# A 4096 x 4096 matmul with bias and tanh by two levels of seven products: returned blocks of the third column in another order, and the last pair's sums in another form

## The chip, the cores and the metric

One core of a Trainium2 chip. The metric is the device time of the kernel in microseconds. The kernel before took 1517.2 us, the median of 3 runs (1516.6 to 1518.86).

## What is computed

```python
def setup_inputs():
    m, k, n = 4096, 4096, 4096
    return {
        "a": np.random.randn(m, k).astype(np.float32),
        "b": np.random.randn(k, n).astype(np.float32),
        "bias": np.random.randn(n).astype(np.float32),
    }

def reference(a, b, bias):
    return np.tanh(np.matmul(a, b) + bias)
```

## The kernel before

**Tiling.** The output is cut into four columns of 1024 (`c` = 0 to 3) and sixteen pairs of row blocks of 128. For a pair and a column, A is a 2 x 2 of quadrants (a11, a12, a21, a22: row block by half of the K axis) and so is B (b11, b12, b21, b22: half of K by half of the column). The product is formed in the way of Strassen and Winograd, with seven products m1 to m7 of half size in place of eight, on sums of quadrants: m2 takes b11, m5 b22, m3 d3, m4 d4, m1 d1, m6 e6, m7 e7 on the right (`PRODUCTS`). Each right operand of a column lies in SBUF as four blocks, 0 to 3, of 512 KB. All operands are fp16, sums are fp32 in eight PSUM banks (named ps), TensorE does the products, VectorE the sums of operands and of results, ScalarE copies, clears of banks and the tanh.

**The second level.** In the columns 2 and 3, `four(n)` takes two pairs at once, p and q, and forms every product but m1 by seven quarter products again. Their right operands, called t1 to t4 and the quarters themselves, are "forms" of 512 KB. For m3, m4, m5 and m7 they stay in SBUF: t3 is written over a quarter, (0, 1), of the operand itself (blocks 0 and 1, the right halves), and what stood there is first moved to DRAM (tiles away_...). For m2 and m6 all forms lie in DRAM and are streamed by GpSimd's queue into a few buffers (the tags b11_1 to b11_3, e6_2, e6_3 and a spare): when `multiply` has used one, `let_go` frees its buffer and `pull_four` issues the next load, which waits for TensorE. Within `four`, `group0`, `group1` and `single` are the quarter products in the order of writing: `single(..., 7)`, `3` and `4` are the last three of a product. `group1` returns two adds (`w`, `w2` or `u`, `u2`) that add a shared third, x or o (an SBUF copy of a PSUM half bank), to the right half banks of p and q.

**Leaving.** The last pair of pairs in column 2 (`leave`) forms m1, m6 and m7 whole, 16 products of 512 columns each, and is followed by two steps of ordinary items of column 2 and then by column 3. For these, what was displaced has to come back: the moved quarters (`move(..., False, ...)`, SyncE's queue, two pieces of 256 KB each, tiles d3, d4, b22 and e7), the blocks of b11 and e6, whose buffers had held forms (`bring_block`, GpSimd's queue, two pieces of 256 KB a block; block 0 of both lies in the tile `side`), and b12 and b21 of the next column (`load_raw`, GpSimd's queue, from the fp16 copy in DRAM, 512 KB a block). The table `BACK` says at which `step(k)` of the leaving pair each is issued: step 1 stands after `group0` of m3 and m4, 5 after m4's last product, 6 after m3's, 8 after `group1` of m2 and m5 and the fetches of a22, 10 after m5's last product, 11 and 12 after the first and second m1, 14 to 17 after m6 and m7 of p and of q, and 18 and on in the slots of the items that follow. Blocks of b11 and e6 that are not in the table come back at once when `let_go` frees their buffer.

**Order.** Every engine runs its instructions in the order of writing, so the place of a line in `four` sets what stands ahead of it on each queue. SyncE's queue carries fetches of A, returned quarters and the stores of results; GpSimd's carries forms, blocks and B. The result buffers `ds` and `s` (two each) are taken anew by `take_d` and `take_c`, which must wait until the store of the pair before has read them. `seed` clears a half bank with ScalarE once VectorE has taken what it held, and the next product adds onto it.

**The last pair.** At the end of column 3 `w2` and `u2` add the third to q's right half bank, `first_half` then adds q's left half of the sum into PSUM and the right half into SBUF, applies tanh and stores; `w`, `take_m6` and `u`, `take_m7` do the same for p with 512 columns; the last two products, `single(n, what, 4)`, are followed by a tanh of q's left half straight from PSUM and its store.

Of the kernel before, what the change touches and what calls it, by code (L numbers as in the profile page):

```python
# [20 lines left out]
ADD = mybir.AluOpType.add  # L21
SUB = mybir.AluOpType.subtract
MUL = mybir.AluOpType.mult
TANH = mybir.ActivationFunctionType.Tanh
# [68 lines left out]


BACK = {
# [3 lines left out]
}  # L99

PLACE = {
# [6 lines left out]
HALF = (ds(0, NB // 2), ds(NB // 2, NB // 2))  # L108
# [14 lines left out]
def kernel(  # L123
# [7 lines left out]
    nc = tc.nc  # L131
# [20 lines left out]
    def tt(out_, in0, in1, op):  # L152
        nc.vector.tensor_tensor(out=out_, in0=in0, in1=in1, op=op)  # L153
# [6 lines left out]
    def bank(n, s, what):  # L160
        two = items[n][2] is not None
        if what == "w":
            return banks[5 + 2 * (n % 2)]
        if what == "z":
            return banks[4 + 2 * (n % 2) + (s if two else 0)]
        return banks[(0 if what == "d" else 2) + (s if two else n % 2)]
# [157 lines left out]
    def by_four(x):  # L324
        return x if len(x.shape) == 4 else x.rearrange("p (a b) m -> p a b m", b=TB)
# [171 lines left out]
    def new_out():  # L497
        return outs.tile([P, NB], fp32, name="o", tag="o")
# [314 lines left out]
    def bring_block(c, name, blk):  # L813
        if (c, name, blk) not in blocks:
            what = {"b11": "m2", "e6": "m6"}[name]
            r, i = divmod(blk, 2)
            to = new_bop(name, blk)
            for j in range(2):
                there = corners[name, blk] if (r, j) == (0, 1) else forms[what, (r, j)][:, ds(i * TB, TB)]
                nc.gpsimd.dma_start(out=to[:, :, HALF[j]], in_=there)  # L820
            return
        nc.gpsimd.dma_start(out=new_bop(name, blk), in_=blocks[c, name, blk])

    owner = {}
    free, held, placed, left_count, homes, returned = [], {}, {}, [0], {}, []
# [9 lines left out]
    def let_go(what, name):  # L835
        tag = held.pop((what, name))
        if returned and not queue and tag != "sum":
            bring_block(returned[0], tag[:-2], int(tag[-1]))
        else:
            free.append(tag)  # L840
        pull_four()

    def half_of(n, what, h):
        return by_four(aset[n][TWO[what][0]])[:, ds(h * TP // TB, TP // TB)]
# [12 lines left out]
    def left(n, what, name):  # L857
        of = {"v2": "v1", "v4": "v2"}.get(name)
        if of:
            assert (what, of) in owner.values()  # L860
            of = by_four(placed[what, of])
        place = by_four(place_for(n, what, name))
        if name == "v1":
            tt(place, half_of(n + 1, what, 0), half_of(n + 1, what, 1), SUB)
        elif name == "v2":
            tt(place, half_of(n, what, 0), of, SUB)
        elif name == "v3":
            tt(place, half_of(n + 1, what, 0), half_of(n, what, 0), SUB)
        else:
            tt(place, half_of(n, what, 1), of, SUB)  # L870
# [28 lines left out]
    def third(src, spread=False):  # L899
        if spread:  # L900
            x = new_out()[:, ds(0, NB // 2)]
        else:
            x = halves.tile([P, NB // 2], fp32, name="x", tag="x")
        nc.scalar.copy(x, src)
        return x

    def group0(n, what):
        p, q = pair_of(n, what)
        multiply(n, what, p[:, HALF[0]], (0, 0), (0, 0))
        nc.scalar.copy(p[:, HALF[1]], p[:, HALF[0]])  # L910
        multiply(n, what, between(n, what), "v1", "t1")

    def group1(n, what, spread=False):
        p, q = pair_of(n, what)
        multiply(n, what, p[:, HALF[0]], (0, 1), (1, 0))
        multiply(n, what, p[:, HALF[1]], "v2", "t2")
        nc.scalar.copy(q[:, HALF[0]], p[:, HALF[1]])
        x = third(between(n, what), spread)
        return (
            lambda: tt(p[:, HALF[1]], p[:, HALF[1]], x, ADD),  # L920
            lambda: tt(q[:, HALF[1]], q[:, HALF[0]], x, ADD),
        )

    def single(n, what, *numbers):
        p, q = pair_of(n, what)
        for i in numbers:
            if i == 3:
                multiply(n, what, p[:, HALF[1]], "v4", (1, 1))
            else:
                multiply(n, what, q[:, HALF[0]], *(("v3", "t3") if i == 7 else ((1, 1), "t4")))  # L930
# [62 lines left out]
    def four(n):  # L993
        c = items[n][0]
        p, q, m = n, n + 1, n + 2
# [4 lines left out]
        st = {i: state.setdefault((i, 0), {}) for i in (p, q)}  # L1000
# [19 lines left out]
        def end(name, i, r, j):  # L1020
            nc.scalar.activation(st[i][name], st[i][name], TANH)
            store(st[i][name], pair[i], r, c, j)
# [24 lines left out]
        def take_m6(i, anew=False, later=False):  # L1047
            tt(st[i]["s"], st[i]["s"], bank(i, 0, "w"), ADD)
            if anew:
                seed(i, "w", 0)  # L1050
            if later:
                left_over.append(lambda: end("s", i, 1, 1))
            else:
                end("s", i, 1, 1)

        def take_m7(i, anew=False, later=False):
            tt(st[i]["ds"], st[i]["ds"], bank(i, 0, "z" if leave else "d"), SUB)
            if anew:
# [21 lines left out]
        w, w2 = group1(n, "m4")  # L1080
# [3 lines left out]
        u, u2 = group1(n, "m3", True)  # L1084
# [35 lines left out]
        w, w2 = group1(n, "m2")  # L1120
# [9 lines left out]
        u, u2 = group1(n, "m5", True)  # L1130
# [73 lines left out]
        w, w2 = group1(n, "m6")  # L1204
# [6 lines left out]
        u, u2 = group1(n, "m7", True)  # L1211
        if not last:
            fetch(m, "a12")
        less_m1(q)
        left(n, "m7", "v4")
        if last:
            parts = {"m6": ("s", "w", ADD, 1.0, 1), "m7": ("ds", "d", SUB, -1.0, 0)}

            def first_half(what):
                name, at, op, scale, r = parts[what]  # L1220
                o, here = st[q][name], bank(q, 0, at)
                tt(here[:, HALF[0]], here[:, HALF[0]], o[:, HALF[0]], op)
                tt(o[:, HALF[1]], o[:, HALF[1]], here[:, HALF[1]], op)
                nc.scalar.activation(o[:, HALF[1]], o[:, HALF[1]], TANH)
                store_half(o, q, r, 1, nc.sync)

            single(n, "m6", 7)
            w2()
            first_half("m6")
            single(n, "m7", 7)  # L1230
            u2()
            first_half("m7")
            single(n, "m6", 3)
            w()
            take_m6(p)
            single(n, "m7", 3)
            u()
            take_m7(p)
            for what in ("m6", "m7"):
                name, at, op, scale, r = parts[what]  # L1240
                single(n, what, 4)
                o = st[q][name]
                nc.scalar.activation(o[:, HALF[0]], bank(q, 0, at)[:, HALF[0]], TANH, scale=scale)
                store_half(o, q, r, 0, nc.sync if what == "m6" else nc.scalar)
            return
        single(n, "m6", 7)
        w2()
        single(n, "m7", 7)
# [334 lines left out]
    def load_first(m, queue, out_):  # L1583
# [9 lines left out]
        out=ident, in_=ident, compare_op=mybir.AluOpType.is_equal, fill=0.0,  # L1593
# [45 lines left out]
    ends = {}  # L1639
# [94 lines left out]
    for c in range(1, NC):  # L1734
        n = next(n for n in range(len(items)) if items[n][0] == c)
# [55 lines left out]
    for n in partner:  # L1791
# [26 lines left out]
        if by_two(n, "m4"):  # L1818
# [5 lines left out]
            at = 9 if by_two(n, "m6") else 8  # L1824
# [8 lines left out]
    for slot in range(1 - len(ORDER), SLOTS * len(items)):  # L1833
# [14 lines left out]
        for pos, p in PRODUCTS.items():  # L1848
            n, r = divmod(slot - pos, SLOTS)
# [37 lines left out]
```

## Time and profile before

| | us |
|---|---|
| median of 3 runs | 1517.2 |
| the profiled execution | 1517.48 |
| its span | 1515.7 |
| TensorE busy in the span | 1506.1 |
| leaving pair of column 2, from the stores of the pair before to the last whole product | 1056 to 1105 |
| last pair of column 3, from the last sums to the last store | 1506 to 1514 |

In the groups and timelines of the profile a row gives engine, line, operation, the tile written and the tiles read, the shapes (partitions x elements) and the number of instructions; in a timeline the start and the length in us stand first, and in brackets the idle time ahead of it and what ended that. A row of the windows gives, for a stretch of the span, its length and the busy time and number of instructions of PE (TensorE), PEld (its weight loads), DVE (VectorE), ACT (ScalarE) and POOL (GpSimd), then the granted clock of TensorE, the busy share of the sixteen DMA engines and GB/s. SPq and POOLq are the queues in which SyncE and GpSimd issue transfers. Buffer numbers are left out: `b` stands for any block of b11, b12, b21 or b22, `d` for d1, d3 or d4, `e` for e6 or e7, `h` for a left operand of a quarter product, `g` and `form` for forms.

### The profile page before, as it was taken

Reading aid. Unit: us, or ns where it says so; the run is one execution under the profiler, and the core shown is the slowest. Engines: PE = TensorE matmul, PEld = TensorE weight load, DVE = VectorE, ACT = ScalarE, POOL = GpSimd, SP = SyncE. Lnnn points to the kernel's source line nnn. Section 1 sums busy time; section 2 is a strip of 40 time slices with the busy share of each in tenths; the row PEclk is TensorE's granted clock in tenths of the full one; section 3 lists DMA queues with packets and bytes.
Section 4 is the critical chain, followed back from the end, with each engine's and each line's share of the span. In section 5 each row is a group of like instructions: output and inputs, shape, how many; then the busy total and the mean of one; then the engine's idle time right before and its main releaser. Section 6 shows DMA issues by size and latency. Waiting matters only on the chain.

```text
span 1515.7 us, 23996 instructions
## 1 busy us (share of the span) xinstructions
PE 1506.1 (99%) x9101; PEld 889.4 (59%) x9101; DVE 1184.5 (78%) x1646; ACT 380.3 (25%) x830; POOL 494.0 (33%) x889
## 2 busy tenths in 40 slices
PE   9999999999999999999999999999999999999998
PEld 4444444444445566544444578888644458888886
DVE  6789877777876666677787888889658879888888
ACT  4431111111221122111122223333212222333332
POOL 8775443433603231343453311112312121111111
PEclk9999999999999999999999999999999999999999
DMA  9999998999979998999998978898976687888895
GB/s 185 178 208 257 269 261 213 215 214 241 187 219 287 268 277 267 232 253 238 244 172 243 304 269 302 325 339 300 363 251 204 202 285 266 304 307 314 320 337 181
DMA packets 207672, 390.39 MB, mean 258 GB/s; under 512 B 25538, under 2 KB 103874, under 8 KB 207556
## 3 DMA queue, kind: packets, MB, share of 16 engines
q0 software_dynamic: 119616, 203.22, 57.6%
q1 hardware_dynamic: 87268, 185.24, 34.9%
q8 instruction: 71, 1.16, 0.3%
q10 hardware_dynamic: 672, 0.39, 0.1%
q14 instruction: 45, 0.37, 0.1%
HBM read 337.65 MB, written 136.84 MB: 313 GB/s over the span
## 4 chain that ended last, share of the span: by engine, by line
PE 96%; DMA 2%; POOL 1%; DVE 1%; issue 0%; ACT 0%; SPq 0%; DVEq 0%; POOLq 0%
PE ps L478 56%; PE ps L895 26%; PE ps L957 6%; PE ps L1516 5%; PE ps L678 4%; DMA out_dram<-ds 1%; DMA out_dram<-o 1%; DMA b<-in_b_dram 0%; DMA land<-in_a_dram 0%; POOL side L1605 0%; POOL land L1557 0%; DVE ps L153 0%; DVE h L153 0%; POOL first L1585 0%; DVE ds L153 0%
## 5 line engine op out<-in xcount | busy, mean ns | idle before, releaser
L478 PEld LDWEIGHTS <-a 128*128 128x128 f16 x3136 | 306.7, 98 | 365.1 <-DMA a<-scratch 0.5
L478 PE MATMUL ps<-b,a 128*128 128x512 f16 x1092 | 249.2, 379 | 0.1
L895 PEld LDWEIGHTS <-h 128*128 128x128 f16 x2176 | 212.7, 98 | 27.4 <-DVE h L153 0.9
L833 POOL DMA_DIRECT2D form<-form_m x147 | 77.8, 530 | 407.6 <-PE ps L895 365.2
L478 PE MATMUL ps<-d,a 128*128 128x512 f16 x896 | 202.5, 379 | 0.0
L478 PE MATMUL ps<-e,a 128*128 128x512 f16 x876 | 199.3, 379 | 0.0
L278 DVE STREAM_TRANSPOSE a<-nat 128x1024 f16<-128x1024 f16 (+2 forms) x202 | 175.3, 912 | 19.1 <-PE ps L478 17.6
L895 PEld LDWEIGHTS <-a 128*128 128x128 f16 x1632 | 159.6, 98 | 26.5 <-issue 2.1
L478 PE MATMUL ps<-d,s 128*128 128x512 f16 x624 | 141.0, 379 | 0.0
L250 POOL DMA_DIRECT2D nat<-in_a_dram x176 | 93.0, 533 | 132.0 <-DVE a L278 63.6
L478 PEld LDWEIGHTS <-s 128*128 128x128 f16 x816 | 79.9, 98 | 94.1
L381 POOL DMA_DIRECT2D b<-in_b_dram x192 | 103.5, 545 | 84.0 <-DVE a L278 31.0
L153 DVE TENSOR_TENSOR a<-a,a 128x2048 f16<-128x2048 f16 (+1 forms) x103 | 123.9, 1202 | 0.2
L895 PE MATMUL ps<-form,h 128*128 128x256 f16 x848 | 108.1, 273 | 0.1
L153 DVE TENSOR_TENSOR h<-a,h 128x1024 f16<-128x1024 f16 x136 | 92.3, 685 | 12.5 <-PE ps L895 12.3
L502 ACT ACTIVATE o<-ps 128x512 f32<-128x512 f32 x88 | 52.9, 601 | 152.3 <-issue 101.8
L895 PE MATMUL ps<-form,a 128*128 128x256 f16 x672 | 83.6, 273 | 0.1
L957 PE MATMUL ps<-d,a 128*128 128x512 f16 x352 | 79.4, 379 | 0.0
L153 DVE TENSOR_TENSOR ds<-ds,ps 128x512 f32<-128x512 f32 (+1 forms) x100 | 66.8, 679 | 10.6 <-PE ps L957 5.5
L979 ACT CAST ps<-zeros 128x256 f32<-128x256 f16 x140 | 50.1, 380 | 98.7 <-DVE s L153 51.5
L153 DVE TENSOR_TENSOR ps<-ps,x 128x256 f32<-128x256 f32 x90 | 38.7, 430 | 41.9 <-PE ps L895 26.8
L478 PE MATMUL ps<-side,a 128*128 128x512 f16 x272 | 69.8, 379 | 0.0
(196 smaller groups left out, 1934.8 us busy)
## 6 DMA issues: line engine op xcount, KB each, us to landing
form<-form_m POOLq DMA_DIRECT2D x147, 512.0 KB, 7.4
a<-scratch SPq DMA_DIRECT2D x140, 512.0 KB, 7.2
out_dram<-o SPq DMA_DIRECT2D x199, 256.0 KB, 5.8
nat<-in_a_dram POOLq DMA_DIRECT2D x288, 128.0 KB, 6.5
scratch<-a SPq DMA_DIRECT2D x48, 512.0 KB, 6.6
b<-in_b_dram POOLq DMA_DIRECT2D x160, 128.0 KB, 5.6
scratch<-a SPq DMA_DIRECT2D x32, 256.0 KB, 6.2
cast<-in_b_dram POOLq DMA_DIRECT2D x64, 128.0 KB, 9.4
```

The lines of the kernel that those rows point to most:

```text
L153: nc.vector.tensor_tensor(out=out_, in0=in0, in1=in1, op=op)
L250: nc.gpsimd.dma_start(out=tl[ds(q * QP, QP), :, :], in_=src.rearrange("(mb p) k -> p mb k", p=QP),)
L278: nc.vector.transpose(dst[:, ds(b0 * tb, n * tb), :].rearrange("P (b t) (mb p) -> P mb b t p", t=tb, p=QP), src[:, :, ds(b0, n), :].rearra ...
L381: nc.gpsimd.dma_start(out=dst[ds(q * QP, QP), ds(t, nt)], in_=src)
L478: nc.tensor.matmul(st[where], at, bt, start=(what == "m2" or n < LEAD and what == "m1") and i == 0, stop=i == len(ts_) - 1, skip_group_che ...
L502: nc.scalar.activation(o, src, TANH)
L678: nc.tensor.matmul(to, at, bt, start=False, stop=t == TP - 1, skip_group_check=True)
L833: nc.gpsimd.dma_start(out=rights[what, name], in_=forms[what, name])
L895: nc.tensor.matmul(to, at, bt, start=False, stop=t == TP - 1, skip_group_check=True)
L957: nc.tensor.matmul(to[:, half], at[:, t // TB, t % TB], bop[right, t // TB][:, t % TB, half], start=anew and t == 0, stop=t == T - 1, skip ...
L979: nc.scalar.copy(bank(n, 0, where)[:, HALF[half]], zeros)
L1516: nc.tensor.matmul(mb[m % 4, j], aq[m, kt // T][:, kt % T, :], right(kt, j), start=fresh and kt == k0, stop=stop and kt == k1 - 1, skip_gr ...
```

## The change

The table gets other steps, and two more entries, blocks 2 and 3 of b11, which `let_go` therefore no longer brings back by itself. In the last pair the shared thirds, kept in a dictionary, are added by GpSimd to the right halves of the sums in SBUF, for q and p, ahead of the last products; p's left halves are added by themselves, early; and the adds that remain take only the half bank that the last product wrote.

```diff
 BACK = {
-    ("m4", "t3"): 5, ("m3", "t3"): 12, ("m7", "t3"): 1,
-    ("b12", 0): 12, ("b12", 1): 12, ("b21", 0): 18, ("b21", 1): 18,
-    ("b11", 0): 6, ("e6", 0): 2, ("e6", 1): 5, ("m5", "t3"): 12,
+    ("m4", "t3"): 17, ("m3", "t3"): 16, ("m7", "t3"): 8,
+    ("b12", 0): 17, ("b12", 1): 17, ("b21", 0): 19, ("b21", 1): 19,
+    ("b11", 0): 9, ("e6", 0): 6, ("e6", 1): 7, ("m5", "t3"): 10, ("b11", 2): 10, ("b11", 3): 11,
 }
...
     def let_go(what, name):
         tag = held.pop((what, name))
         if returned and not queue and tag != "sum":
-            bring_block(returned[0], tag[:-2], int(tag[-1]))
+            name, blk = tag[:-2], int(tag[-1])
+            if (name, blk) not in BACK:
+                bring_block(returned[0], name, blk)
         else:
             free.append(tag)
...
+    thirds = {}
+
...
-        x = third(between(n, what), spread)
+        x = thirds[what] = third(between(n, what), spread)
...
         less_m1(q)
-        left(n, "m7", "v4")
         if last:
-            parts = {"m6": ("s", "w", ADD, 1.0, 1), "m7": ("ds", "d", SUB, -1.0, 0)}
+            ends = {"m6": ("s", "w", ADD, 1.0, 1), "m7": ("ds", "d", SUB, -1.0, 0)}
+            near, far = HALF
+            for what, (name, at, op, scale, r) in ends.items():
+                for i in (q, p):
+                    o = st[i][name][:, far]
+                    nc.gpsimd.tensor_tensor(out=o, in0=o, in1=thirds[what], op=op)
+
+            def take(what, i, half, src):
+                name, at, op, scale, r = ends[what]
+                tt(st[i][name][:, half], st[i][name][:, half], src, op)
+
+            for what, (name, at, op, scale, r) in ends.items():
+                take(what, p, near, bank(p, 0, at)[:, near])
+                if what == "m6":
+                    left(n, "m7", "v4")
+            for what, (name, at, op, scale, r) in ends.items():
                 o, here = st[q][name], bank(q, 0, at)
-                tt(here[:, HALF[0]], here[:, HALF[0]], o[:, HALF[0]], op)
-                tt(o[:, HALF[1]], o[:, HALF[1]], here[:, HALF[1]], op)
-                nc.scalar.activation(o[:, HALF[1]], o[:, HALF[1]], TANH)
+                single(n, what, 7)
+                take(what, q, far, here[:, near])
+                tt(here[:, near], here[:, near], o[:, near], op)
+                nc.scalar.activation(o[:, far], o[:, far], TANH)
                 store_half(o, q, r, 1, nc.sync)
-
-            single(n, "m6", 7)
-            w2()
-            first_half("m6")
-            single(n, "m7", 7)
-            u2()
-            first_half("m7")
-            single(n, "m6", 3)
-            w()
-            take_m6(p)
-            single(n, "m7", 3)
-            u()
-            take_m7(p)
-            for what in ("m6", "m7"):
-                name, at, op, scale, r = parts[what]
+            for what, (name, at, op, scale, r) in ends.items():
+                single(n, what, 3)
+                take(what, p, far, bank(p, 0, at)[:, far])
+                end(name, p, r, r)
+            for what, (name, at, op, scale, r) in ends.items():
                 single(n, what, 4)
                 o = st[q][name]
-                nc.scalar.activation(o[:, HALF[0]], bank(q, 0, at)[:, HALF[0]], TANH, scale=scale)
+                nc.scalar.activation(o[:, near], bank(q, 0, at)[:, near], TANH, scale=scale)
                 store_half(o, q, r, 0, nc.sync if what == "m6" else nc.scalar)
             return
+        left(n, "m7", "v4")
```

TensorE's instructions and their order are the same in both kernels. The queues show what the table moves. On SyncE's queue, at the start of the leaving pair (out_0_dram is a store of the pair before, away_m7 and away_m4 are returned quarters), before:

```order
L493 DMA out_0_dram<-ds_9201 128x512
L493 DMA out_0_dram<-ds_9189 128x512
L493 DMA out_0_dram<-s_9226 128x512
L644 DMA e7_0_6535<-away_m7_2_t3_6891 128x4x256
L644 DMA e7_1_6567<-away_m7_2_t3_6891 128x4x256
L644 DMA d4_0_6513<-away_m4_2_t3_6856 128x4x256
L644 DMA d4_1_6537<-away_m4_2_t3_6856 128x4x256
L312 DMA a22_9828<-scratch_15_107 128x1024
```

and with the change:

```order
L493 DMA out_0_dram<-ds_9201 128x512
L493 DMA out_0_dram<-ds_9189 128x512
L493 DMA out_0_dram<-s_9226 128x512
L312 DMA a22_9822<-scratch_15_107 128x1024
L312 DMA a22_9822<-scratch_14_106 128x1024
L312 DMA a22_9827<-scratch_15_107 128x1024
L312 DMA a22_9827<-scratch_14_106 128x1024
L644 DMA e7_0_6535<-away_m7_2_t3_6891 128x4x256
L644 DMA e7_1_6567<-away_m7_2_t3_6891 128x4x256
```

m7's quarter moved behind the four fetches of a22; m4's stands 20 rows further down, behind the last store of `ds`, m3's four rows ahead of it, and m5's between the stores of m5's results.

On GpSimd's queue in the same place (form_9595 is the last form whose load the pair before releases, side and e6_1 are blocks 0 and 1 of e6), before:

```order
L833 DMA form_9595<-form_m2_4_6824 128x2048
L820 DMA side_108<-form_m6_0_7014 128x4x256
L820 DMA side_108<-corner_e6_0_6984 128x4x256
L820 DMA e6_1_9726<-form_m6_0_7014 128x4x256
L820 DMA e6_1_9726<-corner_e6_1_7047 128x4x256
L833 DMA form_9753<-form_m2_5_6886 128x2048
L833 DMA form_9764<-form_m2_6_6859 128x2048
```

and with the change:

```order
L833 DMA form_9595<-form_m2_4_6824 128x2048
L833 DMA form_9744<-form_m2_5_6886 128x2048
L833 DMA form_9755<-form_m2_6_6859 128x2048
L820 DMA side_108<-form_m6_0_7014 128x4x256
L820 DMA side_108<-corner_e6_0_6984 128x4x256
L820 DMA e6_1_9791<-form_m6_0_7014 128x4x256
L820 DMA e6_1_9791<-corner_e6_1_7047 128x4x256
L820 DMA e6_2_9803<-form_m6_2_7089 128x4x256
```

The two blocks moved behind two forms; further down block 0 of b11 goes behind its block 1, and the next column's b21 behind its first two blocks of b11.

On VectorE at the end of the program (s and ds are the sums in SBUF, 14067 and 14030 p's, 14078 and 14042 q's; h is the last left operand; x and o are the thirds), before:

```order
L153 TENSOR_TENSOR h_10767<-a12_13829,h_10767 128x1024
L153 TENSOR_TENSOR ps_1_248<-ps_1_248,x_14324 128x256
L153 TENSOR_TENSOR ps_1_248<-ps_1_248,s_14078 128x256
L153 TENSOR_TENSOR s_14078<-s_14078,ps_1_248 128x256
L153 TENSOR_TENSOR ps_6_253<-ps_6_253,o_14345 128x256
L153 TENSOR_TENSOR ps_6_253<-ps_6_253,ds_14042 128x256
L153 TENSOR_TENSOR ds_14042<-ds_14042,ps_6_253 128x256
L153 TENSOR_TENSOR ps_3_250<-ps_3_250,x_14324 128x256
L153 TENSOR_TENSOR s_14067<-s_14067,ps_3_250 128x512
L153 TENSOR_TENSOR ps_0_247<-ps_0_247,o_14345 128x256
L153 TENSOR_TENSOR ds_14030<-ds_14030,ps_0_247 128x512
```

and with the change:

```order
L153 TENSOR_TENSOR s_14067<-s_14067,ps_3_250 128x256
L153 TENSOR_TENSOR h_10767<-a12_13829,h_10767 128x1024
L153 TENSOR_TENSOR ds_14030<-ds_14030,ps_0_247 128x256
L153 TENSOR_TENSOR s_14078<-s_14078,ps_1_248 128x256
L153 TENSOR_TENSOR ps_1_248<-ps_1_248,s_14078 128x256
L153 TENSOR_TENSOR ds_14042<-ds_14042,ps_6_253 128x256
L153 TENSOR_TENSOR ps_6_253<-ps_6_253,ds_14042 128x256
L153 TENSOR_TENSOR s_14067<-s_14067,ps_3_250 128x256
L153 TENSOR_TENSOR ds_14030<-ds_14030,ps_0_247 128x256
```

Four adds of x and o have left VectorE; they are the last four instructions of GpSimd, behind its last form. p's left halves stand around the last `h`, and p's two adds of 512 became 256.

More of the change, by code (lines that the diff above doesn't have):

```diff
@@ L1214, in four @@
         less_m1(q)
-        left(n, "m7", "v4")
         if last:
-            parts = {"m6": ("s", "w", ADD, 1.0, 1), "m7": ("ds", "d", SUB, -1.0, 0)}
-            def first_half(what):
-                name, at, op, scale, r = parts[what]
+            ends = {"m6": ("s", "w", ADD, 1.0, 1), "m7": ("ds", "d", SUB, -1.0, 0)}
[4 more added lines that the diff above has]
+                    nc.gpsimd.tensor_tensor(out=o, in0=o, in1=thirds[what], op=op)
@@ L1231, in four @@
-            u2()
-            first_half("m7")
-            single(n, "m6", 3)
-            w()
-            take_m6(p)
-            single(n, "m7", 3)
-            u()
-            take_m7(p)
-            for what in ("m6", "m7"):
-                name, at, op, scale, r = parts[what]
+            for what, (name, at, op, scale, r) in ends.items():
[3 more added lines that the diff above has]
+            for what, (name, at, op, scale, r) in ends.items():
```

## The prediction

> **What bounds the kernel now.** I read the page's head first, then a table of equal windows, then TensorE's waits, and last the timelines of the two places that the diff touches.
>
> ```profile
> span 1515.7 us, 23996 instructions
> PE 1506.1 (99%) x9101; PEld 889.4 (59%) x9101; DVE 1184.5 (78%) x1646; ACT 380.3 (25%) x830; POOL 494.0 (33%) x889
> ...
> 1040.00:1080.00 40.00, 38.40 (x329) 31.87 (x328) 31.07 (x50) 13.05 (x36) 12.82 (x20) 1.00 0.99 349
> 1080.00:1120.00 40.00, 39.73 (x200) 19.21 (x198) 20.41 (x30) 7.93 (x14) 8.40 (x14) 1.00 1.01 352
> ...
> 1480.00:1520.00 40.00, 30.33 (x247) 23.88 (x244) 28.75 (x46) 9.95 (x25) 4.23 (x8) 0.95 0.50 171
> ...
> PE ps L895 <- ACT ps L979: 1.5, 1, 1.5
> ```
>
> TensorE is busy 1506.1 of 1515.7 us at a granted clock of 1.00, and the change leaves its instructions and their order as they were. So a gain can come only from TensorE's gaps. After the opening, nearly all of them lie in two places: 1.60 + 0.27 us in the third column's leaving pair (1040 to 1120), and the tail, where TensorE ends near 1510.33 and the span at 1515.7. Both parts of the diff sit exactly there.
>
> **The leaving pair: what is lost there.** A busy share hides the slow restart of a pipelined TensorE, so I measure the loss against the pair one earlier, which runs the same products in the same order. Rows of that pair, then of the leaving pair:
>
> ```profile
> 1013.33 1.04 PE L895 MATMUL ps<-d,a 128*128 128x256 f16 x8
> 1027.34 1.04 PE L895 MATMUL ps<-b,a 128*128 128x256 f16 x8
> 1037.82 3.62 PE L957 MATMUL ps<-d,a 128*128 128x512 f16 x16
> ...
> 1056.95 1.04 PE L895 MATMUL ps<-d,a 128*128 128x256 f16 x8
> 1072.63 1.03 PE L895 MATMUL ps<-b,a 128*128 128x256 f16 x8 [1.51 <-ACT ps L979]
> 1083.89 7.07 PE L957 MATMUL ps<-d,a 128*128 128x512 f16 x32
> ```
>
> From the first of these groups to the last the earlier pair takes 1037.82 - 1013.33 = 24.49 us and the leaving pair 1083.89 - 1056.95 = 26.94. The loss is 2.45 us, 1.67 of it before m5's first product (15.68 against 14.01), the rest in restarts and in a late VectorE behind it. Why was m5 late?
>
> ```profile
> 1057.28 3.76 SPq L493 DMA_DIRECT2D out_dram<-ds  x2
> 1061.72 2.34 SPq L644 DMA_DIRECT2D e<-away_m_t  x2
> 1065.11 5.08 SPq L644 DMA_DIRECT2D d<-away_m_t  x2
> ...
> 1057.28 14.11 DMA out_dram<-ds
> ...
> 1024.32 0.69 DVE L153 TENSOR_TENSOR ds<-ps,bias_bc 128x512 f32<-128x512 f32 x1
> 1071.48 0.69 DVE L153 TENSOR_TENSOR ds<-ps,bias_bc 128x512 f32<-128x512 f32 x1 [3.66 <-DMA out_dram<-ds]
> ...
> 1024.00:1026.00 2.00, 2.00 (x21) 1.80 (x19) 1.87 (x5) 0.58 (x2) 0.00 (x0) 1.00 0.11 43
> 1068.00:1070.00 2.00, 2.00 (x21) 1.79 (x20) 0.00 (x0) 0.00 (x0) 0.32 (x1) 1.00 1.03 377
> ```
>
> VectorE's take_d needs a `ds` buffer whose store to DRAM was issued at 1057.28 and took 14.11 us. ScalarE clears the bank behind take_d, m5 waits for the clearing. One pair earlier the same add starts at 1024.32; moved by the distance of the pairs (1056.95 - 1013.33 = 43.62) that is 1067.94, and here it is 1071.48. The last two rows (busy times, then clock, DMA share, GB/s) show why: at that point the earlier pair's DMA engines have run dry (0.11), here they are full (1.03), with four quarters on SyncE's queue and the four pieces of e6's blocks 0 and 1 on GpSimd's, 8 x 256 KB.
>
> **Step 1, the table BACK.** It moves just these eight out of the time before 1069: m7's quarter behind the fetches of a22, m4's and m3's behind the m7 products, e6's blocks behind the last two forms, and those wait for TensorE:
>
> ```profile
> 1069.68 0.55 POOL L833 DMA_DIRECT2D form<-form_m  x1 [7.79 <-PE ps L895]
> ```
>
> Between 1057 and 1069 the queues then hold what they held one pair earlier, so I take the earlier pair as the price: take_d at about 1068, no gap, **2.45 us gained**. Bounds: nothing, if the store is as slow without them; above, 2.6, since a later start is at stake too:
>
> ```profile
> 1090.80 1.03 PE L957 MATMUL ps<-side,a 128*128 128x512 f16 x4
> 1098.57 6.21 PE L957 MATMUL ps<-e,a 128*128 128x512 f16 x28
> 1104.80 1.04 PE L478 MATMUL ps<-side,a 128*128 128x512 f16 x4
> 1100.17 1.84 SPq L312 DMA_DIRECT2D a<-scratch  x4
> ```
>
> 32 products of this form run in 6.91 us (1083.89 to 1090.80, where the next group starts), so 28 should end at 1104.61; the next starts 0.19 late, on a21, fetched only at 1100.17. Two quarters stood ahead of that fetch on SyncE and are now behind it. I count nothing for it.
>
> What is late next? Eight 256 KB pieces now go out after 1069.7, beside what already went there. The first users stand 2.45 us earlier than now, and a product of 16 takes 3.45: e6's block 0 at 1088.35 (1090.80 - 2.45), e7 with m7's quarter one product on at 1091.8, b11 at 1102.3 (1104.80 - 2.45), m5's quarter one product on at 1105.8, d3 at 1109.3, d4 two on at 1116.2. Issues, by the earlier pair's rows plus 43.62 and this pair's less 2.45: e6's blocks by about 1077, m7's quarter at 1077 behind the a22 fetches (1031.34 + 2.06 one pair earlier), m3's near 1098 and m4's near 1105, each behind a store of `ds`. That fetch, and landings in this stretch (KB each, median us to landing):
>
> ```profile
> 1031.34 2.06 SPq L312 DMA_DIRECT2D a<-scratch  x2
> ...
> b<-form_m POOLq DMA_DIRECT2D x4, 256.0 KB, 7.8
> d<-away_m_t SPq DMA_DIRECT2D x1, 256.0 KB, 14.6
> ```
>
> At 8 us all have 2 us or more to spare; at the worst seen, 14.6 us (a quarter waiting at 1063 to 1067), m7's quarter is 0.3 us late and m3's and m4's about 3. On SyncE m5's quarter gains a wait for m5's products on the block that it overwrites; they end before m1 starts, and SyncE comes to it only behind the stores of m2 and m5, so a11's fetch and the stores queued behind it lose nothing. On GpSimd b21 for the next column now stands behind a block that waits for TensorE near 1105; VectorE first adds it only here, 30 us later:
>
> ```profile
> 1141.90 1.22 DVE L153 TENSOR_TENSOR d<-side,b 128x2048 f16<-128x2048 f16 x1
> ```
>
> **Step 2, the last pair.** Rows of the tail as it is:
>
> ```profile
> 1508.42 1.91 PE L895 MATMUL ps<-form,a 128*128 128x256 f16 x16
> ...
> 1506.07 0.43 DVE L153 TENSOR_TENSOR ps<-ps,x 128x256 f32<-128x256 f32 x1 [0.25 <-PE ps L895]
> 1510.13 0.69 DVE L153 TENSOR_TENSOR ds<-ds,ps 128x512 f32<-128x512 f32 x1
> ...
> 1510.86 0.63 ACT L1021 ACTIVATE ds<-ds 128x512 f32<-128x512 f32 x1 [0.43 <-DMA out_dram<-ds]
> 1511.39 0.36 ACT L1243 ACTIVATE s<-ps 128x256 f32<-128x256 f32 x1
> 1511.65 0.38 ACT L1243 ACTIVATE ds<-ps 128x256 f32<-128x256 f32 x1
> 1512.06 0.36 ACTq L1015 DMA_DIRECT2D out_dram<-ds  x1
> ```
>
> VectorE runs ten adds from 1506.07 to 1510.82 without a pause, and that, not the transfer that the row names, frees ScalarE at 1510.86: the add of `ds` ends 0.04 before. TensorE's last product ends at 1508.42 + 1.91 = 1510.33, but its activation starts at 1511.65 because two of 512 columns stand ahead of it. The change takes four adds of 0.43 off this run, makes two of 0.69 into 0.43, and puts two near halves ahead of it, beside VectorE's last `h`, where it waits for TensorE; six adds of 0.43 remain behind 1506. They then end 0.5 after the last far product, near 1509.1, ScalarE's wide activations by 1509.7, and the last one starts with TensorE's end, at 1510.36. Gain 1511.65 - 1510.36 = **1.29 us**.
>
> The four GpSimd adds have no row. Beside ScalarE's two copies, on which they wait, the nearest is
>
> ```profile
> 1503.65 0.38 ACT L904 COPY x<-ps 128x256 f32<-128x256 f32 x1
> 1505.40 0.38 ACT L904 COPY o<-ps 128x256 f32<-128x256 f32 x1
> 2.31 0.33 POOL L1592 TENSOR_SCALAR_AFFINE_SELECT ident<-ident 128x128 f16<-128x128 f16 x1
> ```
>
> a select over half the elements with one input. Below, 0.43 (VectorE's price); above 4 x 0.33 = 1.32 (twice elements, twice inputs); I take 0.66, by elements. `x` is copied by 1504.03 and `o` by 1505.78, so at 0.66 the adds end near 1504.8, 1505.4, 1506.4 and 1507.1, each before VectorE wants it (1505.97, 1506.84, 1507.7, 1508.6). At 1.32 the last ends near 1509.4, VectorE's last at 1509.85, and 0.7 of the 1.29 is left. Above, 1.6: the last stores no longer crowd together. Behind the adds GpSimd has nothing left but the end. The Trainium skill (GPSIMD Engine Reference, 3.1 Elementwise) speaks against the move: a two-input add on GpSimd takes 1.96 times VectorE's time, 4497 ns for 2048 elements, an estimate of 0.56 us for 256. By it the sum would be the same, since the adds are off the path until 1.0 us each; no run so far shows one.
>
> **Sum.** 2.45 + 1.29 = 3.74 us. The profiled execution took 1517.48 (1.78 around its span) and would take 1513.74; that is 0.28 above the median, so from the median 1517.2 it is **1513.5 us**.
>
> **Rivals.**
> (a) The moved loads are late in part: m7's quarter, a21 or m3's quarter stalls TensorE by 0.5 to 2.5 us in all. For it: 12 to 14.6 us landings in a full queue. Against it: two 512 KB loads of b21 leave the same stretch. 1514 to 1516, about 1515.
> (b) The table does not do what it says: store and take_d are late anyway, from the fetches at 1047 to 1057. Against it: the earlier pair has those too. Only the tail gains: 1515.9.
> (c) GpSimd's first add is slow to start. Nothing for it in the trace, where the first select takes 0.33. If it ends X after 1504.1, the last activation ends at about 1507.9 + X, so the tail gains nothing from X = 4.1 and the kernel from X = 6.6. At 6: 1516.6. The same page of the Trainium skill (2.1 Instruction dispatch) puts the first call of freshly loaded code at about 6 us; no load stands ahead of the adds in the program.
> (d) Slower: GpSimd's queue. The program lets each transfer there wait for the eighth before it, and this wait shows in
>
> ```profile
> 1087.52 0.53 POOL L371 DMA_DIRECT2D b<-cast  x1 [0.91 <-DMA b<-corner_b]
> ```
>
> e6's block 3 now waits for the form issued at 1069.7 to land and then has to land itself: two landings of L after 1069.7, wanted at 1090.9. At 8 us it is there at 1085.7; above L = 10.6 TensorE stalls, above 12.5 the 3.74 us are spent. At 14.6 it comes at 1098.9, 8 us late: 1521.5.
>
> **How the numbers follow.** Forecast 0.66, (a) 0.14, (b) 0.05, (c) 0.05, (d) 0.10. Less than 0.2%, 3.0 us, is about what a measurement of this kernel cannot tell from no change. The forecast's own range, 1512.6 to 1514.4, is nearly all beyond it: faster 0.65. (a) to (c) fall within it: 0.24. Slower 0.11, (d) and what is left of the forecast. The range leaves out (d), (c) at its worst and a little at the lower end: 1512.5 to 1516.2.
>
> **What would show it.** Right: no gap before m5's first product of the leaving pair, take_d to m1 as long as one pair earlier, the DMA share dropping before 1069 and full after; in the tail, four GpSimd adds under 1 us, the last activation within 0.1 of TensorE's end. Wrong: a wait of TensorE for a transfer between 1088 and 1117, or VectorE waiting for GpSimd after 1506.

## The result, and the profile after

The changed kernel took **1524.0 us** (median of 5 runs, 1522.82 to 1525.22) against 1518.37 of the kernel before on the same chip: a ratio of 1.004, 95% interval 1.0025 to 1.0054. It is 5.6 us slower, where 3.7 us faster was forecast. The profiled execution has a span of 1522.6 us, 6.9 above the one before.

TensorE's timeline of the changed kernel in the leaving pair (start, length, and in brackets the idle time ahead and what ended it):

```profile
1057.58 1.04 PE L897 MATMUL ps<-d,a 128*128 128x256 f16 x8
...
1071.59 1.04 PE L897 MATMUL ps<-b,a 128*128 128x256 f16 x8
...
1082.07 7.07 PE L961 MATMUL ps<-d,a 128*128 128x512 f16 x32
1088.97 1.03 PE L961 MATMUL ps<-side,a 128*128 128x512 f16 x4
1089.84 2.75 PE L961 MATMUL ps<-e,a 128*128 128x512 f16 x12
1101.43 5.35 PE L961 MATMUL ps<-e,a 128*128 128x512 f16 x16 [8.84 <-DVE s L153]
1106.62 1.03 PE L961 MATMUL ps<-side,a 128*128 128x512 f16 x4
...
1113.52 1.03 PE L478 MATMUL ps<-side,a 128*128 128x512 f16 x4
```

The first part is what was forecast. From the first group to m1 the way is 1082.07 - 1057.58 = 24.49 us, as one pair earlier, where it was 26.94; m5 (1071.59) starts without a gap. VectorE's `take_d`, which was held up at 1071.48, now waits 0.50 us for the store issued at 1058.00:

```profile
1068.95 0.69 DVE L153 TENSOR_TENSOR ds<-ps,bias_bc 128x512 f32<-128x512 f32 x1 [0.50 <-DMA out_dram<-ds]
```

Then, 21 us after m5's start, comes something new: m1 of p and q (32 products) and m6 of p (16) run, and ahead of m7 of p TensorE stands still for 8.84 us. Its 16 products then take 5.35 us, where 16 take 3.62 elsewhere. From m1 to column 3's first product the way is 1113.52 - 1082.07 = 31.45 us against 20.91 before.

The row names an add into `s` on VectorE. VectorE's timeline shows what held that up, SyncE's what was issued ahead, and a list of the transfers issued from 1082.3 to 1082.5 how long the store took (KB, us to landing):

```profile
1086.30 1.22 DVE L153 TENSOR_TENSOR a<-a,a 128x2048 f16<-128x2048 f16 x1
1100.09 0.69 DVE L153 TENSOR_TENSOR o<-s,ps 128x512 f32<-128x512 f32 x1 [12.57 <-DMA out_dram<-o]
1100.70 1.87 DVE L153 TENSOR_TENSOR s<-s,ps 128x512 f32<-128x512 f32 x3
```

```profile
1075.97 2.90 SPq L312 DMA_DIRECT2D a<-scratch  x4
1078.92 1.46 SPq L644 DMA_DIRECT2D e<-away_m_t  x2
1082.41 8.05 SPq L493 DMA_DIRECT2D out_dram<-o  x3
```

```profile
out_dram<-o SPq DMA_DIRECT2D x1, 256.0 KB, 17.7
```

The same store before (issued at 1084.53):

```profile
out_dram<-o SPq DMA_DIRECT2D x1, 256.0 KB, 7.7
```

`take_m5` of q needs a buffer `o`. The pool has three, and the one whose turn it is holds m2's result of p until its store has read it. That store, issued at 1082.41 behind four fetches of a22 and the two pieces of m7's returned quarter, lands after 17.7 us, at 1100.1. In VectorE's order `take_m1` stands behind the waiting add, and it frees the bank into which m7 of p is to go. The quarter itself, which m7 of p also reads, needs 18.5 us (its first piece; the profile has no landing of the second):

```profile
e<-away_m_t SPq DMA_DIRECT2D x2, 256.0 KB, 18.5
```

The restart is slow as well. Windows of the changed kernel (length, busy time of the engines, TensorE's granted clock, DMA share, GB/s):

```profile
1092.50:1101.40 8.90, 0.09 (x1) 0.10 (x1) 1.31 (x3) 0.54 (x1) 0.00 (x0) 0.63 0.89 315
1101.50:1103.50 2.00, 2.00 (x5) 0.64 (x5) 1.07 (x2) 0.63 (x1) 0.00 (x0) 0.50 0.61 202
1103.50:1105.50 2.00, 2.00 (x7) 0.80 (x6) 0.00 (x0) 0.00 (x0) 0.00 (x0) 0.63 0.87 247
1105.50:1107.50 2.00, 2.00 (x11) 0.90 (x10) 0.69 (x1) 0.00 (x0) 0.00 (x0) 1.00 0.88 320
```

The clock falls to half during the stall and stays there until about 1105.0, 3.6 us behind the restart (the mean of 0.63 from 1103.50 to 1105.50 is 1.5 us at half and 0.5 at full): 5.35 - 3.62 = 1.73 us more.

In the tail TensorE's last group, GpSimd's four adds and ScalarE's last two rows read, each from the timeline of that engine,

```profile
1517.13 1.91 PE L897 MATMUL ps<-form,a 128*128 128x256 f16 x16
```

```profile
1512.82 1.41 POOL L1225 TENSOR_TENSOR s<-s,x 128x256 f32<-128x256 f32 x2 [6.89 <-DVE h L153]
1514.56 1.50 POOL L1225 TENSOR_TENSOR ds<-ds,o 128x256 f32<-128x256 f32 x2 [0.33 <-ACT o L906]
```

```profile
1519.07 0.38 ACT L1249 ACTIVATE ds<-ps 128x256 f32<-128x256 f32 x1 [0.32 <-PE ps L897]
1519.49 0.36 ACTq L1019 DMA_DIRECT2D out_dram<-ds  x1
```

TensorE ends at 1519.04 and the last activation starts 0.03 later; the span ends 3.56 us after TensorE (before: 1515.7 - 1510.33 = 5.37). So the 6.9 us are: -2.45 ahead of m1, +10.54 behind it (31.45 - 20.91), -1.81 in the tail, and +0.63 by which the leaving pair already began later (1057.58 against 1056.95), within the spread of the traces: over the thirteen of this document that start lies between 1056.64 and 1058.03.

### The profile page after: what moved, and what is told of

It reads as the page before. It is cut to its first block, busy times and chain, and to the rows that moved or that the text cites. A ratio compares the mean times of both kernels' runs of the same rounds, so it can differ in the third digit from the quotient of the medians.

```text
span 1522.6 us, 24007 instructions
## 1 busy us (share of the span) xinstructions
PE 1507.8 (99%) x9101; PEld 890.3 (58%) x9101; DVE 1182.2 (78%) x1644; ACT 380.1 (25%) x830; POOL 497.0 (33%) x893
## 4 chain that ended last, share of the span: by engine, by line
PE 97%; DMA 2%; DVE 0%; POOL 0%; ACT 0%; issue 0%; POOLq 0%; ACTq 0%; DVEq 0%
PE ps L478 55%; PE ps L897 27%; PE ps L1523 5%; PE ps L961 5%; PE ps L678 4%; DMA out_dram<-o 2%; DMA side<-in_b_dram 0%; DVE ps L153 0%; POOL first L1592 0%; POOL side L1612 0%; DVE a L153 0%; DVE ds L153 0%; ACT o L502 0%; DVE h L153 0%; DVE s L153 0%
## 5 line engine op out<-in xcount | busy, mean ns | idle before, releaser
L478 PEld LDWEIGHTS <-a 128*128 128x128 f16 x3136 | 306.9, 98 | 364.5 <-issue 0.4
L897 PEld LDWEIGHTS <-a 128*128 128x128 f16 x1632 | 159.6, 98 | 25.3 <-issue 0.9
L961 PEld LDWEIGHTS <-a 128*128 128x128 f16 x416 | 41.1, 99 | 55.0 <-issue 11.6
```

The lines of the kernel that those rows point to most:

```text
L478: nc.tensor.matmul(st[where], at, bt, start=(what == "m2" or n < LEAD and what == "m1") and i == 0, stop=i == len(ts_) - 1, skip_group_che ...
L897: nc.tensor.matmul(to, at, bt, start=False, stop=t == TP - 1, skip_group_check=True)
L961: nc.tensor.matmul(to[:, half], at[:, t // TB, t % TB], bop[right, t // TB][:, t % TB, half], start=anew and t == 0, stop=t == T - 1, skip ...
```

## The experiments

Base is the changed kernel unless said. "Way to m1" is the stretch that is 26.94 before and 24.49 after, "way behind m1" the one of 20.91 and 31.45. Between calls the kernel before measured 1517.85 to 1518.37 us.

**The two parts apart.** First the table and `let_go` alone, with the tail of before.

> The change's table and let_go, the tail of before. If the two parts are independent, the leaving pair does what it does in the changed kernel (no gap ahead of m5, then a stall of 8.8 us ahead of the leaving pair's m7 of p) and the tail keeps its 5.4 us between TensorE's end and the span's: about 1524.0 + 1.8 = 1525.8 us. Rival: the new tail has a cost elsewhere, and without it the kernel is no slower than the changed one, 1524 or below.

Measured: 1525.82 us, ratio 1.0046 (1.0033 to 1.006); ways 24.49 and 31.64, tail 5.25. Then the tail alone:

> The table of before, the change's tail. Independent parts: the last activation starts with TensorE's end, 3.6 us from TensorE's end to the span's end in place of 5.4, and the leaving pair loses its 2.45 us as before: 1518.4 - 1.8 = 1516.6 us. Rival: the tail's gain is noise of landings, under 0.8 us: 1517.6 or more.

Measured: 1516.6 us, ratio 0.9991 (0.9982 to 1.0); ways 26.62 and 21.15, tail 3.57. The parts are independent: the table does all the harm, and the tail brings the 5.37 us of before down to between 3.3 and 3.7 in the nine traces that have it, a gain of 1.7 to 2.1 us, though the ratio of this run does not clear noise.

**Which transfer.** One entry of the table back:

```diff
-    ("m7", "t3"): 8,
+    ("m7", "t3"): 1,
```

> The changed kernel with m7's quarter alone back at step 1. Theory 1 (order on SyncE's own queue: the quarter's two pieces stand ahead of the stores of o, and m7 wants it soon after): the store of o lands in under 11 us, the stall ahead of m7 of p falls under 1 us, 1513.5 to 1515.5 us; if its two pieces already hold up the store of ds at 1058, up to 1 us of the 2.45 is lost again. Theory 2 (the traffic of e6's blocks on GpSimd's queue slows all transfers of the stretch): the store of o still needs over 14 us and the stall stays above 4 us, 1519 us or more.

Measured: **1513.95 us**, ratio 0.9968 (0.9956 to 0.9981). The store of o lands in 8.3 us, VectorE waits 3.24 us for it, which costs nothing, and TensorE has no wait from m1 on:

```profile
1082.39 7.07 PE L961 MATMUL ps<-d,a 128*128 128x512 f16 x32
1089.29 1.03 PE L961 MATMUL ps<-side,a 128*128 128x512 f16 x4
1090.16 6.21 PE L961 MATMUL ps<-e,a 128*128 128x512 f16 x28
1096.20 1.03 PE L961 MATMUL ps<-side,a 128*128 128x512 f16 x4
1097.06 6.21 PE L961 MATMUL ps<-e,a 128*128 128x512 f16 x28
1103.11 1.03 PE L478 MATMUL ps<-side,a 128*128 128x512 f16 x4
```

```profile
1091.08 0.69 DVE L153 TENSOR_TENSOR o<-s,ps 128x512 f32<-128x512 f32 x1 [3.24 <-DMA out_dram<-o]
```

The ways are 24.50 and 20.72. At step 1 the quarter stands on SyncE's queue just behind the stores of `ds` and `s`, is issued from 1062.54 to 1064.44, and nothing follows there until the a22 fetches at 1076.40; it did no harm to the store of `ds`, and it lands in 8.8 us, on the same queue and in the same short runs that take 18.5 us at step 8. This version beats both kernels, by 0.3% the one before. The other suspect, with e6's blocks back instead:

```diff
-    ("e6", 0): 6, ("e6", 1): 7,
+    ("e6", 0): 2, ("e6", 1): 5,
```

> The changed kernel with blocks 0 and 1 of e6 alone back at steps 2 and 5. Theory 1 (order on SyncE's own queue): m7's quarter and the store of o behind it stay late, the stall ahead of m7 of p stays above 5 us, 1520 us or more. Theory 2 (traffic on GpSimd's queue): 1 MB less in the stretch from 1072 to 1085, about 3 us at the 330 GB/s of that stretch, so store and quarter land at least 3 us earlier and most of the stall goes: 1514 to 1518 us.

Measured: 1524.7 us, ratio 1.0038 (1.0025 to 1.0051); the stall is 6.11 us, the quarter lands in 15.0, and the way to m1 is 25.79. So 1 MB less of GpSimd's traffic lets the quarter land 3.5 us sooner after its issue, as theory 2 has it, but most of the stall stays, as theory 1 has it; and 1.30 us of the old loss are back. The mirror, the kernel before with the quarter alone moved:

```diff
-    ("m4", "t3"): 5, ("m3", "t3"): 12, ("m7", "t3"): 1,
+    ("m4", "t3"): 5, ("m3", "t3"): 12, ("m7", "t3"): 8,
```

> The kernel before with one number changed: m7's quarter at step 8. If that entry alone carries the loss, TensorE stalls 5 to 9 us ahead of m7 of p, the time is 1523 to 1527 us. Rival: the loss needs the other moved loads too (e6's blocks beside it), and the time stays within 2 us of before.

Measured: 1525.83 us, ratio 1.0047 (1.0033 to 1.0062), a stall of 6.88 us at the same place. One entry carries the loss in either table.

**Order in the queue, or bytes in the stretch.** The quarter at step 8 again, but on ScalarE's queue:

```diff
-                nc.sync.dma_start(*(there, here) if out_ else (here, there))
+                queue_ = nc.scalar if what == "m7" and not out_ and c == 2 else nc.sync
+                queue_.dma_start(*(there, here) if out_ else (here, there))
```

> The changed kernel, m7's quarter still at step 8, but issued on ScalarE's queue. Theory 1 (order in one queue: what stands behind the quarter's 512-byte pieces on SyncE's queue waits for them): the store of o lands in under 11 us in place of 17.7, VectorE's wait for it falls from 12.6 to under 6 us, and what is left of the stall is the quarter's own lateness: 1514 to 1519 us. Theory 2 (0.5 MB more in this stretch slows everything, whatever its queue): the store still needs over 14 us, the stall stays above 5 us, 1520 us or more.

Measured: 1521.25 us, ratio 1.0021 (1.0011 to 1.003). The store lands in 8.2 us and VectorE's wait falls to 3.11, as theory 1 has it: the order was its trouble. But the stall and the time are in theory 2's range, because the quarter is late by itself. With nothing ahead of it on ScalarE's queue its first piece needs 14.6 us; the second is issued by 1077.74, and TensorE waits for it until 1097.92, in this row:

```profile
1097.92 4.04 PE L962 MATMUL ps<-e,a 128*128 128x512 f16 x12 [5.34 <-DMA e<-away_m_t]
```

The reverse, the four stores of o on ScalarE's queue:

```diff
+        if leave:
+            store_on[0] = nc.scalar
         take_m2(p)
...
             take_m5(q)
+            store_on[0] = nc.sync
```

> The changed kernel, but the leaving pair's four stores of o are issued on ScalarE's queue, past m7's quarter. Theory 1 (order in one queue): the store lands in under 11 us, and TensorE waits only for the quarter, which landed near 1098 where m7 of p wants it near 1092.5: the stall goes from 8.8 to about 5.5 us or, if the queue gets free sooner without the stores, a little less; 1519 to 1521.5 us. Theory 2 (volume): the store is as late as before and the stall stays at 8 us or more, 1523 us or more.

Measured: 1522.03 us, ratio 1.0022 (1.0012 to 1.0031). The store lands in 8.0 us, and TensorE waits 4.27 and 0.76 us for the two pieces of the quarter:

```profile
1095.94 1.86 PE L963 MATMUL ps<-e,a 128*128 128x512 f16 x4 [4.27 <-DMA e<-away_m_t]
1098.56 4.52 PE L963 MATMUL ps<-e,a 128*128 128x512 f16 x12 [0.76 <-DMA e<-away_m_t]
```

The time is half a us above theory 1's range. So two delays lay behind one row of the trace, the late quarter and the store behind it; the store only ended last.

**Why the quarter is slow.** The same bytes in long runs (each piece of the quarter as 2 KB a partition in place of four times 512 bytes):

```diff
+                if what == "m7" and c == 2 and not out_:
+                    here = bop[TWO[what][1], 2 * r + i][:, ds(0, TB // 2)]
+                    there = there.rearrange("p (a x) b -> p a (x b)", x=2)
```

> The changed kernel, m7's quarter at step 8 on SyncE's queue as there, the same 2 x 256 KB, but each piece written as one run of 2 KB a partition in place of four of 512 bytes: the left k halves of e7's blocks 0 and 1 get the bytes and the returned quarter stays unrestored, so that the products of m7 behind it in column 2 are of other data. If the short packets make the quarter slow (theory P), it lands in under 13 us in place of 18.5, the store of o behind it in under 13 in place of 17.7, and the stall of 8.8 us falls below 4: 1514 to 1519 us. If SyncE's queue gets only so many bytes a us beside a full GpSimd queue (theory Q), quarter and store are as late as before, the stall stays above 7 us: 1522 us or more.

Measured: 1519.44 us, ratio 1.0012 (1.0002 to 1.0022); the quarter lands in 13.3 us, the store that VectorE waits for in 13.2, and the stall is 4.35:

```profile
1097.06 5.06 PE L964 MATMUL ps<-e,a 128*128 128x512 f16 x16 [4.35 <-DVE s L153]
```

Each of these just misses theory P's bound (13, 13 and 4), and all are far from theory Q's. So short runs are part of it, some 5 of the 18.5 us; but 13 us is still above the 8.9 of the next run. And short runs on GpSimd's queue:

```diff
-                nc.sync.dma_start(*(there, here) if out_ else (here, there))
+                queue_ = nc.gpsimd if what == "m7" and not out_ and c == 2 else nc.sync
+                queue_.dma_start(*(there, here) if out_ else (here, there))
```

> The changed kernel, m7's quarter at step 8, but issued on GpSimd's queue, where pieces of the same form (256 KB in runs of 512 bytes) land in 7 to 11 us. Theory Q (the share of the queue): the quarter lands in 8 to 12 us, by 1092, the store of o on SyncE's queue in under 11 us; what stalls are left are short, under 2 us: 1513.5 to 1516.5 us. Theory P (short packets are slow as such): it lands in 14 us or more there too, stalls of 3 us or more: 1517 us or more.

Measured: 1515.4 us, ratio 0.9982 (0.9973 to 0.9992). Issued at 1077.6 and 1078.3, with the same short runs in the same stretch, the quarter needs half the time, here beside another piece and a fetch of A on SyncE's queue that were issued then:

```profile
e<-away_m_t POOLq DMA_DIRECT2D x2, 256.0 KB, 8.9
e<-form_m POOLq DMA_DIRECT2D x1, 256.0 KB, 8.3
a<-scratch SPq DMA_DIRECT2D x1, 256.0 KB, 10.0
```

The store lands in 7.6 us, and both waits are gone; TensorE waits 0.66 us for a21 and 0.56 for an add. The bytes and the short runs alone are then not the cause, and the run on ScalarE's queue shows that a place behind a22 is at most a part of it. What is left is that SyncE's queue (and ScalarE's) gets little while GpSimd's is full, and less when its runs are short. What in the queues does this is not shown. The queues' rows in the changed kernel, for what was issued and moved from 1071 to 1092, fit it (packets, MB, share of the engines' time):

```profile
q0 software_dynamic: 1400, 4.70, 74.0%
q1 hardware_dynamic: 1370, 1.47, 24.2%
```

GpSimd's queue (q0) moves 4.70 MB and SyncE's (q1) 1.47 MB with nearly as many packets. The Trainium skill (DMA: Bandwidth & Descriptors, "Queues, rings and completion order") says that a DMA engine takes turns between the queues packet by packet. The two rows fit it but do not test it: in the same stretch of the kernel before SyncE's queue moved 2413 packets and GpSimd's 1367. The same page of the Trainium skill ("Issuing engines are not separate DMA queues") says that issuing on several engines saves only the sequencer's time. For the landing of one transfer that is not so here: the same quarter needed 18.5 us on one queue and 8.9 on another, and the measurement decides.

**What the other entries are for.** The table of before with e6's two blocks alone at their new steps, and the new tail:

```diff
-    ("b11", 0): 6, ("e6", 0): 2, ("e6", 1): 5, ("m5", "t3"): 12,
+    ("b11", 0): 6, ("e6", 0): 6, ("e6", 1): 7, ("m5", "t3"): 12,
```

> The table of before with blocks 0 and 1 of e6 alone at their new steps, the change's tail. If e6's traffic alone held up the store of ds (theory A), the whole 2.45 us comes back: TensorE has no gap ahead of m5, the leaving pair's way to m1 is 24.5 us, 1514 to 1514.8 us. If the quarters of m4 and m7 have their share (theory B, as the 25.8 us of the run with e6 early suggest: 1.3 of the 2.45 with e6 alone, so some 1.1 without it), the way is 25 to 26 us and the time 1515 to 1516.3 us.

Measured: 1519.43 us, ratio 1.0007 (0.9997 to 1.0017). The way to m1 is 24.50: e6's blocks alone bring the whole 2.45 us, as theory A has it. But the time does not come down, for a reason neither theory named, a wait for a21. TensorE's timeline and SyncE's:

```profile
1106.29 1.76 PE L478 MATMUL ps<-side,a 128*128 128x512 f16 x4 [3.81 <-DMA a<-scratch]
```

```profile
1092.93 1.17 SPq L644 DMA_DIRECT2D d<-away_m_t  x2
1094.14 5.03 SPq L644 DMA_DIRECT2D b<-away_m_t  x2
1099.26 2.50 SPq L493 DMA_DIRECT2D out_dram<-s  x1
1101.87 1.85 SPq L312 DMA_DIRECT2D a<-scratch  x4
```

m3's and m5's quarters (d and b) stand ahead of the fetch on SyncE's queue. TensorE now comes 2.3 us earlier to it (m1 starts at 1081.60, before at 1083.89), the fetch is issued 1.7 us later (before: 1100.17), and the 0.19 us of before become 3.81, with a slow restart of 1.7 us behind them. With all the other entries at the change's steps and m7's at step 1 there is no such wait; which of m3's and m5's does it was not tried apart.

**GpSimd in the tail.** The run with m7's quarter early, with the four adds on VectorE behind the last left operand:

```diff
-                    nc.gpsimd.tensor_tensor(out=o, in0=o, in1=thirds[what], op=op)
+                    nc.vector.tensor_tensor(out=o, in0=o, in1=thirds[what], op=op)
```

> The run with m7's quarter early (1513.95 us, 3.57 us from TensorE's end to the span's end), but the four adds of the thirds on VectorE, behind the last left operand, in place of GpSimd. VectorE then has eleven adds of 0.33 to 0.35 us behind it in place of seven: worked out from the rows of that run, its last add ends near 1.3 us later unless it waited before, and ScalarE's last activation starts about 0.3 us behind TensorE's end: 3.9 us, 1514.3 us. If GpSimd carries the whole gain of the tail, 5.2 us or more and 1515.6 us.

Measured: 1514.48 us, ratio 0.9977 (0.9967 to 0.9986); 4.28 us from TensorE's end to the span's end, the last activation 0.17 us behind TensorE. Of the tail's 1.8 us the other form of the sums brings 1.1 and GpSimd 0.7 in these traces. Of the 0.7 only 0.14 are an earlier last activation; the rest is the last store, which takes 3.7 us from its issue to the span's end in place of 3.1, issued 0.13 us behind another in place of 0.56. The medians of the two versions, 1513.95 and 1514.48, do not tell them apart.

## Why the prediction was wrong

- **What bounds the kernel: right.** The loss of 2.45 us was where it was measured, and its cause was the one given: with the eight pieces gone the store of `ds` lands in time, and the way to m1 is that of one pair earlier to 0.01 us. Narrower than said: the four pieces on GpSimd's queue (e6) do it alone, the four on SyncE's are not needed (a way of 24.50 with e6 alone moved and with m7's quarter left early). The four on SyncE's are m7's and m4's quarters in two pieces each, not four quarters; m3's was issued only at 1095.06.
- **"At 8 us all have 2 us or more to spare": wrong, and this is the step that failed.** It took landing times from a group's median (7.8) and a worst case (14.6), and priced the quarter of m7 with them. It was issued at 1078.9 in place of 1077 and took 18.5, so its first piece came at 1097.4 where TensorE wanted it at 1092.6 (1091.8 in the prediction's clock). The median was that of GpSimd's queue; the quarter stood on SyncE's, in short runs, beside a full GpSimd queue. The 1 MB of a22 ahead of it explains a part at most: with nothing ahead, on ScalarE's queue, TensorE still waited 5.34 us for it.
- **The list of users was incomplete.** "A transfer is late" was checked for each moved load and for its reader alone. What stood behind the quarter on its own queue, the stores of o, was not on the list, though the whole loss of the first step was a store that came late and the buffer that it held. The stores cost 8.84 us, more than the quarter (5.3) would have alone, and the slow restart, for which the sum has no term, 1.7 more.
- **"I count nothing for it" (a21): right in the sum, but the reason was missing.** With the other entries at their old steps the fetch cost 3.81 us once the 2.45 were gained, so the whole gain hangs on what stands ahead of it. Of the two quarters only m3's is now behind the fetch; m5's stands ahead of it still, but is issued some 10 us earlier (1085.54 in the run with m7's quarter early, before 1096.09).
- **Rival (a) had the right mechanism for the quarter, at 0.5 to 2.5 us in place of 5.3, and not the store.** Rival (d), the slower one, did not happen: e6's block 3 was there when it was wanted. Rival (b) did not happen, since `take_d` was on time. Rival (c) did not happen either, GpSimd's first add starts and ends like the others.
- **The tail: right, a little small.** 1.29 was forecast, 1.8 came; the last activation starts with TensorE's end as said. The rest is the last store: from its issue to the span's end 3.1 us in place of 3.6, what the upper bound of 1.6 stood for. GpSimd's adds take 0.70 and 0.75 us, forecast were 0.66. The Trainium skill (GPSIMD Engine Reference, 3.1 Elementwise) gave an estimate of 0.56 for them; the trace decides. With the adds on VectorE the last activation started 0.17 us behind TensorE, so nearly all of the 1.29 came without GpSimd.
- **The sum.** With the quarter left where it was, the same working gives 1513.5 and the run measured 1513.95. What was missing is +10.5 us: 8.84 of waiting and 1.73 of slow restart. The sign named for a wrong forecast, a wait of TensorE between 1088 and 1117, showed at 1092.6, with VectorE between it and the transfer.

## What to carry to other kernels

When a transfer is moved, list what stands behind it on its own queue, not only who reads it: stores hold buffers, and an in-order engine that waits for a buffer holds up everything written behind that wait. Price a landing by the queue it stands on and by what the other queues carry at that time, not by the median of a group; a queue that is idle early is the cheap place, even if the data is wanted much later. When a stall is taken away, the next deadline moves up by as much, so each later transfer has to be checked against the new time.

## What the runs showed of the hardware

- **A stall costs more than its length, and the surplus does not follow the length.** With 8.84 us of idle time came 1.73 us of half clock, with 4.35 us (the run with long runs) 5.06 - 3.62 = 1.44, and with 7.97 us (the table alone) 6.40 - 3.62 = 2.78:

```profile
1100.18 6.40 PE L959 MATMUL ps<-e,a 128*128 128x512 f16 x16 [7.97 <-DVE s L153]
```

In the changed kernel the clock was at half from 1094.7, 2.2 us after the last product, to 1105.0, 3.6 us behind the restart; with the table alone from 1095.6 (3.4 after) to 1105.9 (5.7 behind). The Trainium skill (TensorE: Matmul & The Clock Gate, Part 1) gives half clock after some 3.4 us without work and for 3.4 us of work behind it. The seven traces with one stall of over 3 us here lie around these figures, from 2.2 to 4.6 and from 2.6 to 5.7 us; a wait of 1.51 us in the kernel before left the clock at full.
- **A GpSimd add slows a VectorE add of two SBUF operands.** The last `h` takes 0.94 to 0.95 us in the nine traces with the adds on GpSimd, and 0.69 in the four without, the run with them on VectorE among these; adds that read PSUM keep their 0.41. VectorE's timeline of the changed kernel, with such an add just before the GpSimd adds (they start at 1512.82) and one beside them:

```profile
1512.09 0.69 DVE L153 TENSOR_TENSOR h<-a,h 128x1024 f16<-128x1024 f16 x1 [0.46 <-PE ps L897]
...
1513.29 0.41 DVE L153 TENSOR_TENSOR s<-s,ps 128x256 f32<-128x256 f32 x1
1513.83 0.95 DVE L153 TENSOR_TENSOR h<-a,h 128x1024 f16<-128x1024 f16 x1
1514.70 0.41 DVE L153 TENSOR_TENSOR ds<-ds,ps 128x256 f32<-128x256 f32 x1
```
